# Three more seven-product quads in a hybrid attention and SSM block, and one set of operands fetched by another queue

## The chip, the cores and the metric

The kernel runs on one core of a Trainium2 chip. Its time is the device time of one execution in microseconds (us), the median of several runs. The core has a matrix engine (TensorE, PE in the profile; its weight loads are PEld), a vector engine (VectorE, DVE), a scalar engine (ScalarE, ACT), GpSimd (POOL) and SyncE (SP), which here only issues DMA transfers. Each engine works through its own list of instructions in order.

## What is computed

A block with two branches over 256 positions and a model width of 2048, in float32. Shortened from the reference:

```python
hn = rms_norm(x, norm_w)
q, k, v, z_a, z_s, xbc, dt_raw, g_a, g_s = split(hn @ w_in)
o_a = dilated_window_attention(q, k, v) * silu(z_a)      # 16 heads of 128
y   = rms_norm(ssd_scan(conv(xbc), dt_raw) * silu(z_s), ssm_norm_w)
merged = sigmoid(g_a) * (o_a @ w_attn_branch) + sigmoid(g_s) * (y @ w_ssm_branch)
out = rms_norm(x + merged @ w_out, final_norm_w)
```

Attention scores get a bias that grows with the distance between two positions, and the exponentials are weighted by how many of the three window patterns hold a pair: two constant tables, `dist` and `count`.

## The kernel before

Each large product is made of float32 operands that are split in two parts of lower precision, a high and a low one, and of three matmuls: high by high, high by low, low by high. Weights stream from HBM in units of 128x1024 numbers (512 KB) into a ring of five buffers. For a unit `w`, ACT writes the high part `h` (line 278) and DVE the low part `l = w - h` (line 279).

The work runs in stages: gate of the SSM branch, SSM heads and scan (`ps_xs`, `ps_zs`), the SSM branch product (`ps_ssm`), value projection (`ps_v`), 16 attention heads (`ps_q`, `ps_k`, `ps_za`), then the gate of the attention branch (`ps_ga`), the attention branch product (`ps_attn`) and the output product (`ps_out`). The products ssm, v, ga, attn and out are made by `gemm_pair` (line 463 on), in two passes each, named by the columns that they start with, 0 and 2. A pass for ga, attn or v has eight *quads* of two 128-row tiles each. A plain quad takes two units and 24 matmuls of 512 columns. A quad that is listed in `S_QUADS` is made by the seven-product scheme of Strassen and Winograd instead: seven block products of three matmuls, 21 in all. `G_ORDERS`, `V_ORDERS` and `A_ORDERS` give the order of the quads of a pass.

A seven-product quad needs other operands than a plain one:

- a whole unit `wa`, half a unit `wc`, and a table `wt` of block differences, which was made earlier and put into HBM. On ACT there are four high parts, `ha`, `hc`, `htt` and `htu` (line 551). On DVE there are their low parts `la`, `lc`, `ltt`, `ltu` (line 552) and one subtraction in place, `wa - wt` (line 565), which `htu` and `ltu` are made of.
- left factors: sums of blocks of the left operand, split in two. They are made once per quad (`keep_left`), stored in HBM (`spill`, line 242) and fetched back (`fetch_left`, line 441). `sx_x` are those of the input, used by v and ga; `sx_o` are those of the attention output, used by attn. The buffer in which a left factor of the attention output is made, `sxt_o`, has the tag "ht", as has the high part `htu`, and there are two buffers of that tag.

The tables `wt` for ga, attn and out are made during the attention heads by `sum_jobs` (line 244 on): each job loads 768 KB, makes two DVE subtractions of 128x512 (lines 254, 255) and stores 512 KB. Here there are 19 jobs, started at every fourth unit. A small copy by POOL (lines 249, 253, 440) makes a transfer wait for a chosen unit.

All transfers of weights, tables and left factors are issued on SP's queue, in its order. After the eight quads of a pass, `fold` (lines 589 to 594) combines four of the products; for ga, two tanh passes follow, and for attn, DVE adds and scales the results (lines 1155, 1144, 1145), before PE transposes them (`mtp`, line 1137). The order of the instructions on each engine is set by a scheduler, from priorities in the code.

Of the kernel before, what the change touches and what calls it, by code (L numbers as in the profile page):

```python
# [23 lines left out]
KT = D // P  # L24
# [12 lines left out]
DT_LAG, CB_LAG, TURN_LAG, GT_LAG, Y_LAG, S_LAG, M_LAG = 2, 8, 3, 2, 11, 2, 2  # L37
Y_AFTER = 0, 0
GS_BEFORE = {0: (0, 1), 4: (2,)}
A_ORDERS = {0: (0, 1, 2, 4, 3, 6, 5, 7), 2: (0, 2, 1, 4, 3, 5, 6, 7)}  # L40
V_ORDERS = {0: (0, 2, 4, 1, 3, 5, 6, 7), 2: (0, 2, 1, 4, 3, 5, 6, 7)}
G_ORDERS = {c: (0, 2, 1, 4, 3, 5, 6, 7) for c in (0, 2)}
O_LEFT = {0: {0: (0, 3), 4: (1, 5)}, 2: {}}
O_ORDERS = {0: (0, 1, 2, 4, 3, 6, 5, 7), 2: None}
RX_UNITS = {c: 16 + c for c in range(1, 8)}
# [2 lines left out]
NEG = -1.0e30  # L48
S_QUADS = {
    ("ssm", 0): (5, 7, 8, 10, 11, 12, 13), ("ssm", 2): (3, 5, 7, 8, 10, 11, 12, 13),  # L50
    ("v", 0): (2, 3, 4, 5, 6), ("v", 2): (2, 4, 5, 6), ("ga", 0): (2, 4, 5, 6), ("ga", 2): (2, 4, 5, 6),
    ("attn", 0): (2, 4, 6), ("attn", 2): (2, 4, 5, 6), ("out", 0): (3, 5), ("out", 2): (3, 5),
}
Y_ORDERS = {0: (0, 1, 2, 3, 5, 4, 7, 8, 6, 10, 11, 9, 12, 14, 13, 15), 2: (0, 3, 1, 5, 2, 7, 8, 4, 10, 11, 6, 12, 9, 13, 14, 15)}
Y_LATE = {12: 4, 13: 6}
SX_Y = sorted({*S_QUADS[("ssm", 0)], *S_QUADS[("ssm", 2)]}, key=Y_ORDERS[0].index)
Y_SPARE = {q: int(q in S_QUADS[("ssm", 0)] and q in S_QUADS[("ssm", 2)]) for q in SX_Y}
SX_X = (2, 4, 5, 6)
SX_V = (3,)
O_BEHIND = 7, 14, 15, 17  # L60
SUMS_ATT = [(t, q) for t in [(n, c) for n in ("ga", "attn", "out") for c in (0, 2)] for q in S_QUADS[t]]
ATT_QUADS = sorted({*S_QUADS[("attn", 0)], *S_QUADS[("attn", 2)]})
IN_PLACE = {"ssm": [(0, 12), (2, 12)]}
SUMS_SSM = [(t, q) for t in (("ssm", 0), ("ssm", 2), ("v", 0), ("v", 2)) for q in S_QUADS[t] if (t[1], q) not in IN_PLACE.get(t[0], ())]
SUM_UNITS = 2, 9, 16
LEFT_EVERY, ATT_EVERY = 11, 4
SUM_LAG = 3
ROOM_SSM = 2
WHOLE = slice(0, 512)
# [129 lines left out]
def hybrid_block(ctx: ExitStack, tc: tile.TileContext, wall, xt, x, pk_d, cst_d, fw_d, out):  # L199
# [34 lines left out]
    def behind_unit(n, f):  # L234
        on_unit.setdefault(n, []).append(f)
# [56 lines left out]
    def blocks(t, c):  # L292
        return [t[:, i, (c + j) * 512 : (c + j + 1) * 512] for i in range(2) for j in range(2)]
# [140 lines left out]
    def new_sx(pool, bufs, spare, name):  # L434
        return pool.tile([P, 2, 4 - spare, P], F32R, name=f"sx_{name}", tag=f"sx{spare}", bufs=bufs)

    def fetch_left(kept, pool, bufs, key, x, spare, u):
        def get(behind):
            sx = new_sx(pool, bufs, spare, f"{key[0]}{key[1]}")
            gp.tensor_copy(sx[:, 0, 0, 0:1], behind)  # L440
            nc.sync.dma_start(sx.bitcast(F32), lefts[key])
            kept[key[1]] = left_parts(sx, x, spare)

        behind_unit(u, get)
# [140 lines left out]
    def fold(prods, dst):  # L585

        d11, d12, d21, d22 = dst
        p1, p5, p6, p7 = prods
        ac.activation(d11, p1, AF.Copy)
        ac.activation(d22, p5, AF.Copy)  # L590
        ve.tensor_tensor(d12, p6, d11, ALU.add)
        ve.tensor_tensor(d21, p7, d12, ALU.add)
        ve.tensor_tensor(d12, d12, d22, ALU.add)
        ve.tensor_tensor(d22, d21, d22, ALU.add)
# [4 lines left out]
            ac.activation(th[:, i, tag[1] * 512 : tag[1] * 512 + 512], accs[i], AF.Tanh, scale=scales[i])  # L599

    def rsqrt_rows(sums, n, name):
        var = lead.tile([P, 2], F32, name=f"var_{name}", tag="var", bufs=1)
        ve.tensor_scalar(var, sums, 1.0 / n, EPS, ALU.mult, ALU.add)
        r = lead.tile([P, 2], F32, name=f"r_{name}", tag="rr", bufs=1)
        gp.tensor_tensor(r, var, half, ALU.pow)
        hr = lead.tile([P, 2], F32, name=f"hr_{name}", tag="hr", bufs=1)
        ve.tensor_scalar(hr, r, 0.5, None, ALU.mult)
        return r, hr

# [83 lines left out]
    with tc.tile_pool(name="ssm", bufs=2) as sp:  # L693
# [327 lines left out]
    vt = big.tile([P, 2, D], F32, name="vt", tag="yo1a")  # L1021
    th_a = big.tile([P, 2, D], F32, name="th_a", tag="yo1b")
    xl = ctx.enter_context(tc.tile_pool(name="xl", bufs=1))
    dc = xl.tile([P, 768], F32, name="dc", tag="dc")
    dist_c, count_c = dc[:, :384], dc[:, 384:]
    behind_unit(FIRST[("v", 2)] + 1, lambda behind: fetch(dc, cst_d[:, :768], behind))
    room = room_of(big.tile([P, 6 * 512], F32, name="room_v", tag="yo0a"), 2, 2)
    with tc.tile_pool(name="vx", bufs=1) as vx:
        tl = big.tile([P, 4, UNIT], F32R, name="tl_v", tag="yo0b")
        room["tl"] = [(tl[:, 2 * n], tl[:, 2 * n + 1]) for n in range(2)]  # L1030
        for n, q in enumerate(SX_V):
            fetch_left(sx_of_x, vx, len(SX_V), ("x", q), two_kts(XT, q), 0, FIRST[("v", 0)])
        for n, q in enumerate(SX_X[1:]):
            fetch_left(sx_of_x, xl, len(SX_X) - 1, ("x", q), two_kts(XT, q), 0, FIRST[("v", 0)] + 1 + n)
        for c in (0, 2):
            es, prods = gemm_pair(
                ("v", c), lambda kt: XT[:, kt, :], KT, sx_of_x, c == 2, order=V_ORDERS[c], room=room
            )
            dst = blocks(vt, c)
            fold(prods, dst)  # L1040
            for d, e in zip(dst, es):
                ve.tensor_tensor(d, e, d, ALU.add)
    sx_of_o = {}

    with tc.tile_pool(name="att", bufs=2) as ap:
# [4 lines left out]
        def scores(h, q, k, p):  # L1050
            sps = bank("m1", 2, f"sps{h}")
            pe.matmul(sps[:, :P], q[:, :P], k[:, :P], start=True, stop=True)
            pe.matmul(sps[:, P:384], q[:, P:], k, start=True, stop=True)
            t = cpool.tile([P, 384], F32, name=f"t{h}", tag="ssq")
            slope = 2.0 ** (-8.0 * (h + 1) / NH)
            ve.scalar_tensor_tensor(t, dist_c, slope / SCALE, sps[:, :384], ALU.mult, ALU.add)
            st = ap.tile([P, 8], F32, name=f"st{h}", tag="st", bufs=1)
            parts = ((0, P), (P, 384))
            for i, (a, b) in enumerate(parts):
                ve.tensor_reduce(st[:, i : i + 1], t[:, a:b], mybir.AxisListType.X, ALU.max)  # L1060
            ve.tensor_scalar(st[:, 2:4], st[:, 0:2], -SCALE, None, ALU.mult)
# [17 lines left out]
        def mix(h, pT, za):  # L1079
# [204 lines left out]
```

## Time and profile before

| | |
|---|---|
| time, median of 3 runs | 1381.65 us (1379.74 to 1382.66) |
| the profiled execution | 1381.59 us, its span 1379.8 us |
| PE busy | 1368.4 us, 99% of the span |
| DVE busy | 1168.4 us, 85% |
| ACT busy | 836.6 us, 61% |
| POOL busy | 142.5 us, 10% |
| granted TensorE clock | full in all 40 slices of the span |

The profile shows one execution. A busy time is the time in which an engine has an instruction in work. In timelines, an instruction's start and length are given, and in square brackets how long its engine had been idle before it and what ended the idle time. A matmul's length there is its whole latency; matmuls overlap, so their price is the distance between two starts.

### The profile page before, as it was taken

How to read it: one execution, taken by the hardware profiler on the slowest of the kernel's cores; microseconds unless marked ns; L12 is line 12 of the kernel's file. 1: busy time of each engine (PE TensorE's matmuls, PEld its weight loads, DVE VectorE, ACT ScalarE, POOL GpSimd, SP SyncE). 2: the span in 40 equal slices, each digit the busy share in tenths (PEclk: the TensorE clock that was granted, in tenths of full speed). 3: DMA queues.
4: the chain of work that ended last, by engine and by line, in shares of the span. 5: the costliest groups of instructions: out<-in, count | busy, mean ns of one | idle time of the engine just before them, and what ended most of it. 6: DMA issues, size and time to landing. Idle time of an engine off the chain costs nothing.

```text
span 1379.8 us, 20706 instructions
## 1 busy us (share of the span) xinstructions
PE 1368.4 (99%) x7266; PEld 1166.4 (85%) x7266; DVE 1168.4 (85%) x1753; ACT 836.6 (61%) x1306; POOL 142.5 (10%) x226
## 2 busy tenths in 40 slices
PE   9999999999999999999999999999999999999997
PEld 7888888888888888888888888888888888888886
DVE  6897999897899898788989887777877788888997
ACT  7655777675667676666565554454445556655554
POOL 2301111101010100010001001211111000000112
PEclk9999999999999999999999999999999999999999
DMA  9766978778787867578677668888888757875773
GB/s 348 232 193 198 334 261 284 263 245 283 249 278 236 302 200 223 175 240 277 228 259 273 209 218 282 280 275 276 289 288 300 241 163 268 290 224 177 247 271 122
DMA packets 105080, 345.00 MB, mean 250 GB/s; under 512 B 11728, under 2 KB 13712, under 8 KB 104976
## 3 DMA queue, kind: packets, MB, share of 16 engines
q1 hardware_dynamic: 103536, 339.62, 73.7%
q10 hardware_dynamic: 1440, 4.06, 0.8%
q8 instruction: 57, 0.93, 0.3%
q14 instruction: 47, 0.39, 0.1%
HBM read 314.87 MB, written 28.77 MB: 249 GB/s over the span
## 4 chain that ended last, share of the span: by engine, by line
PE 95%; DMA 2%; ACT 1%; issue 1%; DVE 1%; SPq 0%; POOL 0%; POOLq 0%; ACTq 0%; DVEq 0%
PE ps_xs L333 8%; PE ps_zs L333 8%; PE ps_za L333 4%; PE ps_k L333 4%; PE ps_q L333 4%; PE ps_xs L339 4%; PE ps_zs L339 4%; PE ps_ssm L485 3%; PE ps_ssm L486 3%; PE ps_ssm L484 3%; PE ps_q L339 2%; PE ps_k L339 2%; PE ps_za L339 2%; PE ps_gs L421 2%; PE ps_gs L422 2%; PE ps_gs L420 2%
## 5 line engine op out<-in xcount | busy, mean ns | idle before, releaser
L278 ACT ACTIVATE h<-w 128x1024 fp32r<-128x1024 f32 (+1 forms) x398 | 413.8, 1047 | 303.9 <-issue 80.9
L279 DVE TENSOR_TENSOR l<-w,h 128x1024 fp32r<-128x1024 f32 (+1 forms) x398 | 478.8, 1209 | 114.0 <-ACT h L278 110.4
L333 PE MATMUL ps_zs<-XT,h 128*128 128x512 f32 x496 | 172.1, 393 | 0.0
L333 PE MATMUL ps_xs<-XT,h 128*128 128x512 f32 x496 | 171.6, 393 | 0.0
L339 PE MATMUL ps_zs<-XT,l 128*128 128x256 f32 x496 | 134.8, 280 | 0.9 <-DVE l L279 0.9
L339 PE MATMUL ps_xs<-XT,l 128*128 128x256 f32 x496 | 133.7, 277 | 0.0
L333 PEld LDWEIGHTS ps_xs<-XT,h 128*128 128x128 f32 x496 | 91.3, 188 | 19.4
L333 PEld LDWEIGHTS ps_zs<-XT,h 128*128 128x128 f32 x496 | 91.3, 188 | 18.8
L339 PEld LDWEIGHTS ps_zs<-XT,l 128*128 128x128 f32 x496 | 93.3, 188 | 3.7 <-DVE l L279 1.6
L339 PEld LDWEIGHTS ps_xs<-XT,l 128*128 128x128 f32 x496 | 93.2, 188 | 2.1
L333 PE MATMUL ps_q<-XT,h 128*128 128x512 f32 x256 | 91.1, 404 | 0.0
L333 PE MATMUL ps_k<-XT,h 128*128 128x512 f32 x256 | 88.6, 395 | 0.0
L333 PE MATMUL ps_za<-XT,h 128*128 128x512 f32 x256 | 88.4, 394 | 0.0
L551 ACT ACTIVATE ha<-wa 128x1024 fp32r<-128x1024 f32 x43 | 45.4, 1055 | 43.6 <-PE ps_ssm L486 12.9
L339 PE MATMUL ps_q<-XT,l 128*128 128x256 f32 x256 | 68.4, 278 | 0.0
L339 PE MATMUL ps_k<-XT,l 128*128 128x256 f32 x256 | 68.4, 277 | 0.0
L339 PE MATMUL ps_za<-XT,l 128*128 128x256 f32 x256 | 68.4, 277 | 0.0
L792 ACT ACTIVATE gt<-acb,acT 128x128 f32<-128x128 f32 x128 | 44.0, 391 | 28.8 <-DMA acb<-acum_d 27.4
L552 DVE TENSOR_TENSOR la<-wa,ha 128x1024 fp32r<-128x1024 f32 x43 | 52.4, 1219 | 9.3 <-ACT ha L551 9.2
L552 DVE TENSOR_TENSOR ltu<-wa,htu 128x1024 fp32r<-128x1024 f32 x38 | 46.3, 1219 | 15.9 <-ACT htu L551 15.9
L333 PEld LDWEIGHTS ps_k<-XT,h 128*128 128x128 f32 x256 | 47.0, 188 | 9.9
L333 PEld LDWEIGHTS ps_q<-XT,h 128*128 128x128 f32 x256 | 47.1, 188 | 9.7
(688 smaller groups left out, 3315.1 us busy)
## 6 DMA issues: line engine op xcount, KB each, us to landing
w<-in_wall SPq DMA_DIRECT2D x394, 512.0 KB, 4.8
wa<-in_wall SPq DMA_DIRECT2D x43, 512.0 KB, 5.1
th_a<-in_wall SPq DMA_DIRECT2D x19, 512.0 KB, 5.6
sums_at<-in_wall SPq DMA_DIRECT2D x18, 512.0 KB, 4.7
acb<-acum_d SPq DMA_DIRECT2D x32, 256.0 KB, 3.8
t_ssm<-sums_at SPq DMA_DIRECT2D x13, 512.0 KB, 4.8
wt<-t_ssm SPq DMA_DIRECT2D x13, 512.0 KB, 4.7
th_a<-in_wall SPq DMA_DIRECT2D x19, 256.0 KB, 6.2
```

The lines of the kernel that those rows point to most:

```text
L278: ac.activation(h[:, a:b], w[:, a:b], AF.Copy)
L279: ve.tensor_tensor(l[:, a:b], w[:, a:b], h[:, a:b].bitcast(F32), ALU.subtract)
L333: high = pe.matmul(acc, h[:, kk, :], xs_of(kt), start=(kt == 0), stop=False)
L339: low = pe.matmul(acc[:, S:], l[:, kk, :], xs_of(kt)[:, :S], start=False, stop=(kt == KT - 1))
L420: pe.matmul(accs[i], xh, h[:, kk], start=(kt == 0), stop=False)
L421: pe.matmul(accs[i], xh, l[:, kk], start=False, stop=False)
L484: pe.matmul(acc, xh, h, start=start, stop=False)
L485: pe.matmul(acc, xh, l, start=False, stop=False)
L486: pe.matmul(acc, xl, h, start=False, stop=stop)
L551: ac.activation(h, src, AF.Copy)
L552: ve.tensor_tensor(l, src, h.bitcast(F32), ALU.subtract)
L792: ac.activation(g4[:, n, b], acb[:, j, b // 2 * P : b // 2 * P + P], AF.Relu, scale=-1.0, bias=sc[:, h : h + 1],)
```

## The change

- Three more quads go by the seven-product scheme: quad 3 in both passes of ga, and quad 5 in the first pass of attn. The order of the quads in ga becomes 0, 2, 4, 1, 3, 5, 6, 7 (it was 0, 2, 1, 4, 3, 5, 6, 7), which is the order of the first pass of v in both kernels. In the first pass of attn, quad 5 comes ahead of quad 6.
- The left factor of input quad 3 was used by v alone and had a buffer of its own; now it is kept with the others until the end of ga.
- There are 22 `sum_jobs` in place of 19, started at every 3.75 units from unit 3 on (every 4 from unit 7 on before).
- The four fetches of `sx_o` are issued on GpSimd's queue, and the first of them behind an earlier unit of ga's second pass.
- The constant tables of the attention scores lie in places of constants that are no longer needed, in three transfers, in place of one buffer of 768 columns.

```diff
-A_ORDERS = {0: (0, 1, 2, 4, 3, 6, 5, 7), 2: (0, 2, 1, 4, 3, 5, 6, 7)}
+A_ORDERS = {0: (0, 1, 2, 4, 3, 5, 6, 7), 2: (0, 2, 1, 4, 3, 5, 6, 7)}
-G_ORDERS = {c: (0, 2, 1, 4, 3, 5, 6, 7) for c in (0, 2)}
+G_ORDERS = {c: (0, 2, 4, 1, 3, 5, 6, 7) for c in (0, 2)}
...
-    ("v", 0): (2, 3, 4, 5, 6), ("v", 2): (2, 4, 5, 6), ("ga", 0): (2, 4, 5, 6), ("ga", 2): (2, 4, 5, 6),
-    ("attn", 0): (2, 4, 6), ("attn", 2): (2, 4, 5, 6), ("out", 0): (3, 5), ("out", 2): (3, 5),
+    ("v", 0): (2, 3, 4, 5, 6), ("v", 2): (2, 4, 5, 6), ("ga", 0): (2, 3, 4, 5, 6), ("ga", 2): (2, 3, 4, 5, 6),
+    ("attn", 0): (2, 4, 5, 6), ("attn", 2): (2, 4, 5, 6), ("out", 0): (3, 5), ("out", 2): (3, 5),
...
-SX_X = (2, 4, 5, 6)
-SX_V = (3,)
-O_BEHIND = 7, 14, 15, 17
+SX_X = (2, 4, 3, 5, 6)
+O_BEHIND = 3, 14, 15, 17
...
-    def fetch_left(kept, pool, bufs, key, x, spare, u):
+    def fetch_left(kept, pool, bufs, key, x, spare, u, queue=nc.sync):
         def get(behind):
             sx = new_sx(pool, bufs, spare, f"{key[0]}{key[1]}")
             gp.tensor_copy(sx[:, 0, 0, 0:1], behind)
-            nc.sync.dma_start(sx.bitcast(F32), lefts[key])
+            queue.dma_start(sx.bitcast(F32), lefts[key])
...
-    dc = xl.tile([P, 768], F32, name="dc", tag="dc")
-    dist_c, count_c = dc[:, :384], dc[:, 384:]
-    behind_unit(FIRST[("v", 2)] + 1, lambda behind: fetch(dc, cst_d[:, :768], behind))
+    count = lead.tile([P, P], F32, name="count", tag="cw"), cst[:, 512:768]
+    for n, (dst, a) in enumerate(((mask3, 0), (count[0], 384), (count[1], 512))):
+        behind_unit(FIRST[("v", 2)] + n, lambda behind, dst=dst, a=a: fetch(dst, cst_d[:, a : a + dst.shape[-1]], behind))
...
-            SUMS_ATT, range(FIRST[("q", 0)] + 7, N_UNITS, ATT_EVERY),
+            SUMS_ATT, [FIRST[("q", 0)] + 3 + n * 15 // 4 for n in range(len(SUMS_ATT))],
...
-                sx_of_o, xl if n else xk, max(1, n and len(SX_X) - 1), ("o", q), two_kts(oaT, q), 0, FIRST[("ga", 2)] + O_BEHIND[n]
+                sx_of_o, xl if n else xk, max(1, n and len(SX_X) - 1), ("o", q), two_kts(oaT, q), 0, FIRST[("ga", 2)] + O_BEHIND[n], nc.gpsimd
```

PE's list is the same up to quad 2 of ga's first pass, and 9 rows shorter in all. The first place is there: PE at the end of quad 2, whose last two operands are `htu_11637` before and `htu_11660` after (`ha`, `la`, `hc`, `lc` belong to quad 4; `h`, `l` to quad 1; line numbers are one less after the change). Before:

```order
L485 MATMUL pp_ga_0_11615<-la_11710,XT 128x512
L486 MATMUL pp_ga_0_11615<-ha_11709,XT 128x512
L485 MATMUL ps_ga_0_11527<-la_11710,XT 128x512
L486 MATMUL ps_ga_0_11527<-ha_11709,XT 128x512
L485 MATMUL ps_ga_1_11528<-lc_11714,sx_x_7835 128x512
L486 MATMUL ps_ga_1_11528<-hc_11713,sx_x_7835 128x512
L484 MATMUL pp_ga_3_11618<-htu_11637,sx_x_7640 128x512
L484 MATMUL ps_ga_2_11529<-htu_11637,XT 128x512
L485 MATMUL pp_ga_3_11618<-ltu_11638,sx_x_7640 128x512
```

And after:

```order
L484 MATMUL ps_ga_3_11553<-l_11737,XT 128x512
L485 MATMUL ps_ga_3_11553<-h_11736,XT 128x512
L483 MATMUL ps_ga_0_11550<-h_11742,XT 128x512
L483 MATMUL ps_ga_1_11551<-h_11742,XT 128x512
L483 MATMUL ps_ga_3_11553<-h_11742,XT 128x512
L483 MATMUL pp_ga_3_11641<-htu_11660,sx_x_7636 128x512
L483 MATMUL ps_ga_2_11552<-htu_11660,XT 128x512
L484 MATMUL ps_ga_0_11550<-l_11743,XT 128x512
```

From the first matmul behind the last transpose (`ptp`) of the heads, `htu` of quad 2 comes in the 31st place before and in the 25th after.

The second place is DVE at the end of attn's first pass, where the folded products (`fin`) and the operands of the second pass meet. Before, the list reads (`ltt_12693` and all below it that is named `la` or `ltu` belongs to the second pass):

```order
L552 TENSOR_TENSOR ltu_12492<-wa_12474,htu_12491 128x1024
L279 TENSOR_TENSOR l_12519<-w_12516,h_12518 128x1024
L279 TENSOR_TENSOR l_12525<-w_12522,h_12524 128x1024
L591 TENSOR_TENSOR fin<-pp_attn_2_12352,fin 128x512
L279 TENSOR_TENSOR l_12555<-w_12552,h_12554 128x1024
L279 TENSOR_TENSOR l_12561<-w_12558,h_12560 128x1024
L592 TENSOR_TENSOR fin<-pp_attn_3_12353,fin 128x512
L552 TENSOR_TENSOR ltt_12693<-fin,htt_12692 128x1024
```

And after (`ltt_12736` and `la_12727` belong to the second pass):

```order
L278 TENSOR_TENSOR l_12604<-w_12601,h_12603 128x1024
L551 TENSOR_TENSOR ltt_12567<-fin,htt_12566 128x1024
L278 TENSOR_TENSOR l_12685<-w_12682,h_12684 128x1024
L551 TENSOR_TENSOR ltu_12571<-wa_12553,htu_12570 128x1024
L278 TENSOR_TENSOR l_12691<-w_12688,h_12690 128x1024
L590 TENSOR_TENSOR fin<-pp_attn_2_12389,fin 128x512
L1150 TENSOR_TENSOR fin<-ps_attn_0_12308,fin 128x512
L591 TENSOR_TENSOR fin<-pp_attn_3_12390,fin 128x512
L551 TENSOR_TENSOR ltt_12736<-fin,htt_12735 128x1024
L1139 SCALAR_TENSOR_TENSOR th_a<-th_a,fin 128x512
L592 TENSOR_TENSOR fin<-fin 128x512
L551 TENSOR_TENSOR la_12727<-wa_12722,ha_12726 128x1024
```

Before, the low parts of two plain quads stand ahead of the fold; after, the last parts of a seven-product quad do, and the fold and the sums of the pass are woven between the operands of the next one.

The third place is the fetch of the left factors `sx_o`. Before, SP's list has them between weights:

```order
L530 DMA wa_12167<-in_wall 128x1024
L441 DMA sx_o_12097<-sxd_o_9995 128x1024
L534 DMA wc_12169<-in_wall 128x512
L267 DMA w_12210<-in_wall 128x1024
L267 DMA w_12219<-in_wall 128x1024
L267 DMA w_12275<-in_wall 128x1024
L267 DMA w_12281<-in_wall 128x1024
L441 DMA sx_o_12216<-sxd_o_10780 128x1024
L267 DMA w_12314<-in_wall 128x1024
```

After, they stand in POOL's list, each behind its small copy:

```order
L439 CAST sx_o_12091<-h_12087 128x1
L440 DMA sx_o_12091<-sxd_o_10005 128x1024
L439 CAST sx_o_12253<-h_12249 128x1
L440 DMA sx_o_12253<-sxd_o_10794 128x1024
L439 CAST sx_o_12262<-h_12258 128x1
L440 DMA sx_o_12262<-sxd_o_11191 128x1024
```

Four transfers have left SP's list, and what stands behind them there no longer comes after the copies by POOL.

## Rows read from the trace of the kernel before

**Rows 1.** The page: busy time, share of the span and instructions of each engine.

```profile
PE 1368.4 (99%) x7266; PEld 1166.4 (85%) x7266; DVE 1168.4 (85%) x1753; ACT 836.6 (61%) x1306; POOL 142.5 (10%) x226
```

**Rows 2.** Waits of PE over the whole span: us in total, times, longest.

```profile
PE warm L631 <- DVE ssq L628: 1.4, 1, 1.4
PE ps_zs L339 <- DVE l L279: 0.9, 2, 0.8
PE ps_first L385 <- ACT h L278: 0.7, 2, 0.4
```

**Rows 3.** Chain that ended last, gate's second pass: start, us, what.

```profile
1169.55 0.68 PE ps_ga L484 x3
```

**Rows 4.** Windows: stretch, then us, PE, PEld, DVE, ACT, POOL busy, PEclk, DMA share, GB/s.

```profile
745.10:786.10 41.00, 41.00 (x183) 33.95 (x182) 36.98 (x40) 23.59 (x28) 3.29 (x3) 1.00 0.71 247
...
800.00:1126.80 326.80, 326.80 (x1862) 285.40 (x1861) 250.69 (x465) 165.64 (x250) 43.83 (x57) 1.00 0.78 261
1126.80:1165.00 38.20, 38.20 (x172) 31.68 (x171) 32.23 (x33) 22.03 (x27) 0.00 (x0) 1.00 0.76 248
1165.00:1206.20 41.20, 41.20 (x184) 34.12 (x183) 36.81 (x40) 27.77 (x33) 2.12 (x4) 1.00 0.87 306
1206.20:1247.00 40.80, 40.80 (x182) 33.80 (x181) 35.14 (x40) 20.84 (x24) 0.00 (x0) 1.00 0.68 213
```

**Rows 5.** DVE's timeline, gate's first pass: start, us, line, operation, idle before.

```profile
1134.65 2.35 DVE L279 TENSOR_TENSOR l<-w,h 128x1024 fp32r<-128x1024 f32 x2
1136.92 1.22 DVE L552 TENSOR_TENSOR ltu<-wa,htu 128x1024 fp32r<-128x1024 f32 x1
1138.06 1.22 DVE L552 TENSOR_TENSOR la<-wa,ha 128x1024 fp32r<-128x1024 f32 x1
1139.20 0.68 DVE L552 TENSOR_TENSOR lc<-wc,hc 128x512 fp32r<-128x512 f32 x1
1139.80 1.22 DVE L552 TENSOR_TENSOR ltt<-th_a,htt 128x1024 fp32r<-128x1024 f32 x1
1140.93 1.22 DVE L565 TENSOR_TENSOR wa<-wa,th_a 128x1024 f32<-128x1024 f32 x1
```

**Rows 6.** ACT's timeline there: `htu` of quad 2.

```profile
1131.16 1.06 ACT L551 ACTIVATE htu<-wa 128x1024 fp32r<-128x1024 f32 x1 [3.04 <-DMA sxd_o<-sxt_o]
```

**Rows 7.** PE's timeline there: the first matmul that reads `htu` of quad 2.

```profile
1133.58 0.39 PE L484 MATMUL pp_ga<-htu,sx_x 128*128 128x512 f32 x1
```

**Rows 8.** SP's timeline there: the store of the last left factor of o.

```profile
1126.73 0.33 SPq L242 DMA_DIRECT2D sxd_o<-sxt_o  x1
```

**Rows 9.** ACT's timeline at the start of attn's second pass.

```profile
1249.80 1.04 ACT L551 ACTIVATE htu<-wa 128x1024 fp32r<-128x1024 f32 x1
```

**Rows 10.** PE's timeline there: the first matmul that reads this `htu`.

```profile
1251.67 0.40 PE L484 MATMUL ps_attn<-htu,oaTa 128*128 128x512 f32 x1
```

**Rows 11.** The page: DVE groups of the sum jobs, busy us, mean ns, idle before.

```profile
L254 DVE TENSOR_TENSOR th_a<-th_a 128x512 f32<-128x512 f32 x19 | 13.2, 693 | 1.5
L255 DVE TENSOR_TENSOR th_a<-th_a 128x512 f32<-128x512 f32 x19 | 13.1, 690 | 0.4
```

**Rows 12.** DMA issues in 1165 to 1206.2: count, KB each, median us to landing.

```profile
w<-in_wall SPq DMA_DIRECT2D x10, 512.0 KB, 5.8
...
sx_o<-sxd_o SPq DMA_DIRECT2D x4, 512.0 KB, 6.0
```

**Rows 13.** Waits of SP's queue, 1120 to 1210: us in total, times, longest.

```profile
SPq L441 <- POOL sx_o L440: 5.0, 3, 2.3
```

**Rows 14.** POOL's timeline from gate's second pass on: start, us, operation, idle before.

```profile
1188.67 1.24 POOL L440 CAST sx_o<-h 128x1 fp32r<-128x1 f32 x1 [11.37 <-ACT h L278]
...
1198.48 0.18 POOL L440 CAST sx_o<-h 128x1 fp32r<-128x1 f32 x1 [7.43 <-PE pp_ga L486]
1279.90 3.16 POOL L646 COPY fin<-h 128x1 f32<-128x1 f32 x1 [81.25 <-ACT h L278]
```

**Rows 15.** SP's timeline: the first fetch of a left factor of o.

```profile
1177.33 0.33 SPq L441 DMA_DIRECT2D sx_o<-sxd_o  x1
```

**Rows 16.** PE's timeline: the first matmul that reads one.

```profile
1213.14 0.39 PE L484 MATMUL ps_attn<-hc,sx_o 128*128 128x512 f32 x1
```

More of the change, by code (lines that the diff above doesn't have):

```diff
@@ L65 @@
 SUM_UNITS = 2, 9, 16
-LEFT_EVERY, ATT_EVERY = 11, 4
+LEFT_EVERY = 11
 SUM_LAG = 3
@@ L601, in rsqrt_rows @@
     def rsqrt_rows(sums, n, name):
-        var = lead.tile([P, 2], F32, name=f"var_{name}", tag="var", bufs=1)
+        rows = lead.tile([P, 3, 2], F32, name=f"rows_{name}", tag="rows", bufs=1)
+        var, r, hr = rows[:, 0], rows[:, 1], rows[:, 2]
         ve.tensor_scalar(var, sums, 1.0 / n, EPS, ALU.mult, ALU.add)
-        r = lead.tile([P, 2], F32, name=f"r_{name}", tag="rr", bufs=1)
         gp.tensor_tensor(r, var, half, ALU.pow)
-        hr = lead.tile([P, 2], F32, name=f"hr_{name}", tag="hr", bufs=1)
         ve.tensor_scalar(hr, r, 0.5, None, ALU.mult)
@@ L916, in left_x @@
             keep_left(("x", q), two_kts(XT, q), 0, at)
-        for n, q in enumerate(SX_X + SX_V):
+        for n, q in enumerate(SX_X):
             behind_unit(begin + 3 + n * LEFT_EVERY, lambda behind, q=q: left_x(q, behind))
@@ L1023, in hybrid_block @@
     xl = ctx.enter_context(tc.tile_pool(name="xl", bufs=1))
-    dc = xl.tile([P, 768], F32, name="dc", tag="dc")
-    dist_c, count_c = dc[:, :384], dc[:, 384:]
-    behind_unit(FIRST[("v", 2)] + 1, lambda behind: fetch(dc, cst_d[:, :768], behind))
+    count = lead.tile([P, P], F32, name="count", tag="cw"), cst[:, 512:768]
+    for n, (dst, a) in enumerate(((mask3, 0), (count[0], 384), (count[1], 512))):
+        behind_unit(FIRST[("v", 2)] + n, lambda behind, dst=dst, a=a: fetch(dst, cst_d[:, a : a + dst.shape[-1]], behind))
     room = room_of(big.tile([P, 6 * 512], F32, name="room_v", tag="yo0a"), 2, 2)
[L1028 to L1042, printed above, removed]
+    tl = big.tile([P, 4, UNIT], F32R, name="tl_v", tag="yo0b")
+    room["tl"] = [(tl[:, 2 * n], tl[:, 2 * n + 1]) for n in range(2)]
+    for n, q in enumerate(SX_X[1:]):
+        fetch_left(sx_of_x, xl, len(SX_X) - 1, ("x", q), two_kts(XT, q), 0, FIRST[("v", 0)] + n)
+    for c in (0, 2):
+        es, prods = gemm_pair(
+            ("v", c), lambda kt: XT[:, kt, :], KT, sx_of_x, c == 2, order=V_ORDERS[c], room=room
+        )
+        dst = blocks(vt, c)
+        fold(prods, dst)
+        for d, e in zip(dst, es):
+            ve.tensor_tensor(d, e, d, ALU.add)
     sx_of_o = {}
@@ L1055, in scores @@
             slope = 2.0 ** (-8.0 * (h + 1) / NH)
-            ve.scalar_tensor_tensor(t, dist_c, slope / SCALE, sps[:, :384], ALU.mult, ALU.add)
+            ve.scalar_tensor_tensor(t, mask3, slope / SCALE, sps[:, :384], ALU.mult, ALU.add)
             st = ap.tile([P, 8], F32, name=f"st{h}", tag="st", bufs=1)
@@ L1065, in scores @@
                 ve.scalar_tensor_tensor(
-                    p[:, a:b], p[:, a:b], 1.0, count_c[:, a:b], ALU.mult, ALU.mult,
+                    p[:, a:b], p[:, a:b], 1.0, count[i], ALU.mult, ALU.mult,
                     accum_out=st[:, 4 + i : 5 + i],
```

## The prediction

> **What bounds the kernel now.** I began with the busy times of the page: PE is busy for 1368.4 us, 99% of the span, DVE for 85% [rows 1]. The question is then whether PE's work has gaps. The list of PE's waits has 3.0 us in the whole span, 1.4 us on the sum of squares and 1.6 us on split weights, none of it in value, gate, attention or output products [rows 2]. The windows say the same of the three passes that the change touches: in 1126.8 to 1247 PE is busy for all of each window, at full clock [rows 4]. So here the time of a stage is its number of matmuls times their distance. The chain of work that ended last gives that distance: three matmuls of 512 columns in 0.68 us, 0.2267 us each [rows 3].
>
> DVE is the engine behind it. In the three windows it is busy for 32.23 of 38.20, 36.81 of 41.20 and 35.14 of 40.80 us [rows 4], so it stands idle for 5.97, 4.39 and 5.66 us. A matmul removed is worth its 0.2267 us only as long as the operands of the next still come in time. That is what has to be costed.
>
> **The change part by part.** The profiled execution took 1381.59 us, 1.8 us more than its span and 0.06 under the median, so the sum made against it stands for the median too.
>
> *Matmuls.* A plain quad has 24 and a seven-product quad 21. Three quads change: 9 matmuls less, 9 x 0.2267 = 2.04 us. PE's list is shorter by exactly these 9 rows. If no operand comes late, this is the whole gain.
>
> *DVE.* Two low parts of a plain quad take from 1134.65 to 1136.92, 2.27 us. In a seven-product quad, `la`, `lc` and `ltt` take from 1138.06 to 1140.93, 2.87 us, and `wa - wt` and `ltu` 1.14 us each (the distance from `ltu` at 1136.92 to the next start): 5.15 us [rows 5]. Each of the three quads thus adds 2.88 us to DVE and takes 0.68 us from PE. In the windows that leaves DVE idle for 5.97 - 2.88 - 0.68 = 2.41 us in gate's first pass, 0.83 in its second and 2.10 in attention's first. It still fits, barely in gate's second pass. In gate's new order three seven-product quads follow each other (3, 5, 6): DVE 3 x 5.15 = 15.45, PE 3 x 4.76 = 14.28 us, so DVE falls back by 1.17 us in them. The nearest row is the first pass of v, which has the same five quads in the same order: DVE 36.98 of 41.00 us, PE busy throughout [rows 4]. It kept 4.02 us of idle time, more than any of the three will have, so it speaks for the change without settling it.
>
> *Quad 2 of gate's first pass.* This is the tightest place that I found. `htu` runs from 1131.16 to 1132.22 on ACT, and ACT had stood 3.04 us before it until the store of the last left factor of o had landed, since both use a buffer of tag "ht" [rows 6]. PE reads it at 1133.58 [rows 7], a lead of 1.36 us. After the change its place is the 25th and not the 31st, six matmuls or 1.36 us earlier: PE comes at 1132.22, and the lead is nought. The store is issued at 1126.73 [rows 8] behind a split that stands behind the same DVE work after the change, so it has no reason to move. It took some 4.4 us; were it to take the 5.8 us that a weight takes in a crowded window [rows 12], PE would stand for 1.4 us. Bounds 0 to 1.4, and I take 0.2, since the store's own row is the nearest.
>
> *Gate's second pass.* In its crowded window weights take 5.8 us to land [rows 12], and only 0.83 us of DVE's idle time remain. If none of DVE's idle time there can be used, because each piece of it stands before something that was late, the pass loses 2.88 + 0.68 = 3.56 us less a lead such as the 1.36 us above: bounds 0 to 2.2. I take 0.4, nearer to v's pass, which lost nothing.
>
> *End of attention's first pass.* Quad 5 now is a seven-product quad next to the end, and the fold is woven between the second pass's operands. Before, `htu` of the second pass is done at 1250.84 [rows 9] and read at 1251.67 [rows 10], a lead of 0.83 us. By the same reckoning the bounds are 0 to 3.56 - 0.83 = 2.73; I take 0.4, since 2.10 us of idle time remain.
>
> *Sum jobs.* Three more of them are 3 x (0.693 + 0.690) = 4.1 us on DVE [rows 11] over a stretch where it is idle for 76 of 326.8 us [rows 4], with three stores and six loads. Nothing on PE's path; if that cover were gone, 4.1 us. The three added tables must be read back as well: that is in the load of the windows, 0.25 MB a quad.
>
> *Left factors by GpSimd.* SP's queue stood 5.0 us at three of these fetches, with weights queued behind [rows 13]; PE had no wait there, so freeing it gives back nothing by itself, only slack in the gate's second pass. What a fetch issued by GpSimd costs no row shows. POOL's last copy for them is at 1198.48, and its next work at 1279.90 [rows 14], so what the queue takes itself is hidden; fetches took 6.0 us [rows 12], and the first of these factors, asked for at 1177.33 [rows 15], is first read at 1213.14 [rows 16], 36 us later, so several us more are hidden. Bounds: nothing, or DVE held back as long as the longest of these small POOL instructions, 1.24 us [rows 14], four times, 5.0 us. I take nothing.
>
> By the Trainium skill, DMA: Bandwidth & Descriptors, Issuing engine by pattern, fetches by Sync are "generally faster" than by GpSimd, with a first byte some 0.4 us earlier by its specifications; the sum would be the same by it, since 36 us lie between. No run here shows it yet.
>
> *Tables and constants* move three small transfers and no arithmetic: nothing, with cover of the whole v pass.
>
> Sum: 1381.59 - 2.04 + 0.2 + 0.4 + 0.4 = 1380.55, as a number 1380.5 us; with no stall at all 1379.55.
>
> **The rivals.**
>
> *DVE's idle time cannot be used (slower).* Place: the three passes. In each, DVE's chain grows by 2.88 us and PE's shrinks by 0.68; if the idle time stays where it is, each pass loses 3.56 us less the lead that it had: 10.68 - 1.36 - 1.36 - 0.83 = 7.1 us. Time: 1381.59 - 2.04 + 7.1 = 1386.7. It decides against the change from 2.04 us of stalls on, and measurably from 4.8 us. For it: idle of only 0.83 us in the second gate window, and waits there on DMA and buffers, as before `htu`. Against it: v's first pass with the same quads, without a wait.
>
> *GpSimd's fetches hold DVE (slower).* 5.0 us as above less the 0.83 us left idle: 1380.55 + 4.2 = 1384.7. For it, that nothing in this trace has been issued so; against it, that POOL's small copies lie beside running DVE work without a mark on it.
>
> The Trainium skill, GPSIMD Engine Reference, SBUF interfaces, speaks against the change here: GpSimd shares them with VectorE, which suffers when it reads two SBUF inputs, as every low part does. How long descriptor work would hold it, no run shows.
>
> *More than the matmuls (faster).* The two waits of `ps_zs`, 0.9 us [rows 2], lie in the heads where left factors and their store move. If they vanish and nothing stalls: 1381.59 - 2.04 - 0.9 = 1378.65, over 0.2%. Against it: nothing in the change aims at them.
>
> That the change doesn't do what it says is left out: PE's list is 9 rows shorter.
>
> **How the numbers follow.** Less than 0.2% (2.76 us) can't be told from no change here. Forecast, stalls of 0 to 2.7 us, 1379.5 to 1382.3: 0.67, within 0.2%. Idle time that cannot be used, in whole or from 4.8 us on: 0.15, and GpSimd's fetches: 0.05; both slower. More than the matmuls, or a median of three that falls low (the runs before spread over 2.9 us): 0.13, faster. So faster 0.13, same 0.67, slower 0.20. The range goes from 1378.6, the faster rival, to 1385.5, which takes in the second rival and the lower half of the first.
>
> **What would show it.** Right: PE's waits in the new trace stay near 3.0 us plus 1.0, all three windows have PE busy throughout, shorter by 0.68 us each, DVE's idle time in them falls to some 2.4, 0.8 and 2.1 us, and `htu` of quad 2 is read as soon as it is done. Wrong: waits of PE on `ltu`, `la` or `l` of over 2 us in a pass (the first rival); low parts longer than 1.23 us around 1172 to 1200 (the second); a wait on `sx_o`; or waits in the attention heads, where the sum jobs lie.

## The result, and the profile after

The changed kernel takes 1386.74 us, the median of 6 runs (1384.70 to 1388.11), against 1381.72 us (1379.74 to 1382.66) for the kernel before. The ratio is 1.0037, with a 95% interval of 1.0026 to 1.0047: slower by 5.0 us, where 1.2 us less was forecast. The time lies outside the range that was given (1378.6 to 1385.5), and next to the first rival's 1386.7.

The page of the profiled execution (1386.18 us, span 1384.2) begins with the engines' busy times, as [rows 1]; the second line is the new DMA queue in its part 3 (packets, MB, share).

```profile
PE 1368.9 (99%) x7257; PEld 1164.5 (84%) x7257; DVE 1181.0 (85%) x1768; ACT 841.6 (61%) x1312; POOL 155.4 (11%) x241
...
q0 software_dynamic: 576, 2.10, 0.4%
```

PE has its 9 instructions less (7257 for 7266), and four fetches, 2.10 MB, now go by another kind of queue. The list of PE's waits, as [rows 2], tells where the loss is:

```profile
PE ps_attn L484 <- DVE l L278: 1.7, 1, 1.7
PE warm L629 <- DVE ssq L626: 1.4, 1, 1.4
PE ps_first L384 <- ACT h L277: 1.2, 2, 0.8
PE ps_attn L483 <- ACT hc L550: 1.2, 1, 1.2
PE ps_out L483 <- ACT fin L588: 0.7, 1, 0.7
PE ps_zs L338 <- DVE l L278: 0.7, 1, 0.7
PE ps_attn L483 <- ACT h L277: 0.4, 1, 0.4
```

Four of these are new: three on operands of the attention product, one at the start of the output product. Next come the windows, as [rows 4], with one more for the start of attn's second pass:

```profile
1126.80:1165.00 38.20, 38.13 (x171) 31.25 (x170) 34.63 (x36) 24.75 (x29) 0.00 (x0) 1.00 0.76 245
1165.00:1206.00 41.00, 40.98 (x181) 33.62 (x180) 38.85 (x42) 28.40 (x34) 13.60 (x8) 1.00 0.90 311
1206.00:1247.00 41.00, 41.00 (x182) 33.95 (x182) 35.86 (x38) 24.38 (x29) 0.00 (x0) 1.00 0.70 224
1247.00:1262.00 15.00, 11.67 (x56) 8.62 (x55) 13.30 (x18) 5.56 (x7) 0.00 (x0) 1.00 0.49 176
```

In the gate's passes and in attention's first pass PE is busy throughout, as before. Then, in 15 us around the start of attention's second pass, it is idle for 3.3 us. DVE's idle time in the three passes is 3.57, 2.15 and 5.14 us, where 2.4, 0.8 and 2.1 were forecast: in attention's first pass DVE has hardly more to do than before, and in the 15 us behind it, it is busy for 13.30.

Why the operands are late there is told by DVE's timeline. Where does the first of the folds begin (line 591 before, 590 after)? Before:

```profile
1230.76 0.68 DVE L591 TENSOR_TENSOR fin<-pp_attn,fin 128x512 f32<-128x512 f32 x1
```

After, with the instruction ahead of it, and the two low parts for which PE waits:

```profile
1236.81 1.22 DVE L278 TENSOR_TENSOR l<-w,h 128x1024 fp32r<-128x1024 f32 x1
1239.80 0.69 DVE L590 TENSOR_TENSOR fin<-pp_attn,fin 128x512 f32<-128x512 f32 x1 [1.77 <-PE pp_attn L485]
...
1250.55 2.35 DVE L278 TENSOR_TENSOR l<-w,h 128x1024 fp32r<-128x1024 f32 x2
```

A fold needs the last product of the last seven-product quad. Before, that quad was the third from the end, so most of fold and merge found room while PE worked on two plain quads. Now it is the second from the end: the fold begins 9.0 us later, after DVE has stood for 1.77 us, and then DVE is busy without a gap up to the late `l`, with the 4 folds, 4 sums, 3 of the 8 merges (lines 1139 and 1140 after the change) and the next pass's operands. PE reads the first `l` at 1251.81, when it is just done.

The second wait comes about in another way, which the chain that ended last shows (start, us, what):

```profile
1254.03 1.04 DVE th_a L1139 x2
1255.08 4.92 DMA fin<-in_wall
...
1260.10 0.64 ACT hc L550
```

The half unit `wc` of the second pass is loaded into 512 columns of `fin`, where a result of the first pass lies until it is merged (line 1139). The late merge makes a late transfer, and PE waits for `hc`.

The third place is ACT's timeline at the end of attention:

```profile
1283.33 1.05 ACT L550 ACTIVATE htu<-wa 128x1024 fp32r<-128x1024 f32 x1
1286.52 0.35 ACTq L645 DMA_DIRECT2D fin<-in_x  x1
1286.91 0.60 ACT L588 ACTIVATE fin<-pp_attn 128x512 f32<-128x512 f32 x1 [2.54 <-POOL fin L644]
```

ACT's copy in the fold of the second pass now stands behind a transfer of `x` that ACT issues itself, and that one waits for a small copy by POOL. Before, the copy stood ahead of it. The output product needs the bank that the copy empties.

The distances between PE's starts, less the usual one of the instruction, give the sum: 2.04 us less for nine matmuls; 4.2 us more at the boundary between attention's passes (1.90, 1.40 and 0.72 on the three waits above, 0.20 on a `lc`); 0.9 at the start of the output product; 0.4 in two waits in the gate; 0.6 at the very start, where the first weights came later; 0.8 in small pieces; 0.5 less at the end. Together 4.4 us, the difference of the two spans.

### The profile page after: what moved, and what is told of

It reads as the page before. It is cut to its first block, busy times and chain, and to the rows that moved or that the text cites. A ratio compares the mean times of both kernels' runs of the same rounds, so it can differ in the third digit from the quotient of the medians.

```text
span 1384.2 us, 20755 instructions
## 1 busy us (share of the span) xinstructions
PE 1368.9 (99%) x7257; PEld 1164.5 (84%) x7257; DVE 1181.0 (85%) x1768; ACT 841.6 (61%) x1312; POOL 155.4 (11%) x241
## 4 chain that ended last, share of the span: by engine, by line
PE 93%; DMA 2%; issue 2%; DVE 1%; ACT 1%; POOL 0%; SPq 0%; POOLq 0%; ACTq 0%; DVEq 0%
PE ps_xs L332 8%; PE ps_zs L332 8%; PE ps_za L332 4%; PE ps_k L332 4%; PE ps_q L332 4%; PE ps_xs L338 4%; PE ps_zs L338 4%; PE ps_ssm L484 3%; PE ps_ssm L485 3%; PE ps_ssm L483 3%; PE ps_q L338 2%; PE ps_k L338 2%; PE ps_za L338 2%; PE ps_gs L420 2%; PE ps_gs L421 2%; PE ps_gs L419 2%
## 5 line engine op out<-in xcount | busy, mean ns | idle before, releaser
L277 ACT ACTIVATE h<-w 128x1024 fp32r<-128x1024 f32 (+1 forms) x392 | 407.9, 1047 | 302.8 <-issue 67.2
L278 DVE TENSOR_TENSOR l<-w,h 128x1024 fp32r<-128x1024 f32 (+1 forms) x392 | 471.8, 1209 | 105.7 <-ACT h L277 102.7
L550 ACT ACTIVATE ha<-wa 128x1024 fp32r<-128x1024 f32 x46 | 48.6, 1057 | 51.4 <-DMA wa<-in_wall 10.2
L551 DVE TENSOR_TENSOR la<-wa,ha 128x1024 fp32r<-128x1024 f32 x46 | 56.1, 1219 | 13.4 <-ACT ha L550 13.2
L551 DVE TENSOR_TENSOR ltu<-wa,htu 128x1024 fp32r<-128x1024 f32 x41 | 50.0, 1219 | 11.3 <-ACT htu L550 11.3
```

The lines of the kernel that those rows point to most:

```text
L277: ac.activation(h[:, a:b], w[:, a:b], AF.Copy)
L278: ve.tensor_tensor(l[:, a:b], w[:, a:b], h[:, a:b].bitcast(F32), ALU.subtract)
L550: ac.activation(h, src, AF.Copy)
L551: ve.tensor_tensor(l, src, h.bitcast(F32), ALU.subtract)
```

## The experiments

Each was timed beside the kernel before on the same chip; ratios are against it, with 95% intervals. Waits that are given *by PE's starts* are such distances. Theory A says that the loss is at the end of attention's first pass, by the place of its last seven-product quad. The letters of the rivals are in the expectations, and "..." in an edit stands for the part of a line that stays.

### The attention quad taken back (two samples)

```diff
-A_ORDERS = {0: (0, 1, 2, 4, 3, 5, 6, 7), ...
+A_ORDERS = {0: (0, 1, 2, 4, 3, 6, 5, 7), ...
...
-    ("attn", 0): (2, 4, 5, 6), ...
+    ("attn", 0): (2, 4, 6), ...
```

> The changed kernel with the first pass of attn as it was before the change (quads 2, 4, 6 by seven products, 5 plain, order 6, 5, 7 at its end); the rest of the change stays, so 6 matmuls less than before, 1.36 us. Theory A (all that matters is at the end of attn's first pass): the waits of PE of 4.2 us at 1248 to 1262 and the one of 0.9 us at the start of out vanish, and the time is 1381.7 - 1.4 + 0.4 (the two small waits in gate) = 1380.7. Theory B (what costs is in gate or the GpSimd fetches or the sum jobs, and the wait in attn is only where it shows): the waits move but stay, 1384 to 1387.

> The same kernel as in the first experiment (gate's quads and GpSimd's fetches, attn's first pass as before), once more beside the kernel before, for a narrower interval: six matmuls less, 1.36 us, and one wait of 0.2 us in gate; ratio 0.9992 if nothing else is lost.

1381.06 us, ratio 0.9995 (0.9987 to 1.0004), and the second time 1381.73 us, 0.9996 (0.9987 to 1.0005). PE's waits in the second sample are all:

```profile
PE warm L629 <- DVE ssq L626: 1.4, 1, 1.4
PE ps_first L384 <- ACT h L277: 0.9, 2, 0.7
```

No wait in attention is left, nor the one at the output product, in either sample. The loss of 5 us hangs on this one quad. Six matmuls less should give 1.36 us; by their ratios both samples lie on that side, by 0.5 to 0.7 us, and neither is clear of no change. That this kernel beats the one before isn't shown.

### The attention quad alone

```diff
-A_ORDERS = {0: (0, 1, 2, 4, 3, 6, 5, 7), ...
+A_ORDERS = {0: (0, 1, 2, 4, 3, 5, 6, 7), ...
...
-    ("attn", 0): (2, 4, 6), ...
+    ("attn", 0): (2, 4, 5, 6), ...
```

> The kernel before with one edit: quad 5 of attn's first pass by seven products, ahead of quad 6, with its one sum job; 3 matmuls less than before, 0.68 us. Theory A: this edit alone makes the loss, PE waits of 4 to 5 us on l and hc at the start of attn's second pass, 1385 to 1386. Theory B: no more than 1382.

1384.38 us, ratio 1.0021 (1.0012 to 1.0030). Its waits in attention:

```profile
PE ps_attn L484 <- ACT htu L551: 1.2, 1, 1.2
PE ps_attn L484 <- ACT hc L551: 1.0, 1, 1.0
...
PE ps_attn L485 <- DVE l L279: 0.2, 1, 0.2
```

The same place, and the same two ways, at a smaller size than expected: 1.0021 is 2.9 us, and the time lies below Theory A's 1385 to 1386. The edit is slower by itself, without gate, left factors or queue. The rest of the loss comes only in the company of the other parts: by PE's starts the boundary costs 3.0 us here and 4.2 in the changed kernel, and the wait at the output product isn't here.

### Two plain quads last

```diff
-A_ORDERS = {0: (0, 1, 2, 4, 3, 5, 6, 7), ...
+A_ORDERS = {0: (0, 1, 2, 4, 5, 6, 3, 7), ...
```

> The changed kernel with the same four seven-product quads in attn's first pass, but in the order 0, 1, 2, 4, 5, 6, 3, 7: two plain quads behind the last seven-product one and not one. Theory A1 (the place of the last seven-product quad matters, since the fold can't start before it and its results must be merged before the second pass gets its buffers for wc): the fold starts some 5.4 us earlier against the end of the pass, the waits of 4.2 us fall below 1 us, 1381 to 1383. Theory A2 (five more DVE operations in the pass, wherever they stand): the waits stay, within 1 us of the changed kernel, 1386 to 1387.5.

1384.38 us, ratio 1.0019 (1.0010 to 1.0029): between the two expectations, some 2.4 us better than the changed kernel and 2.6 worse than the one before. By PE's starts the waits at the boundary are 2.1 us in place of 4.2. The fold begins at 1237.82 and not at 1239.80, 2 us earlier and not 5.4. These are DVE's timeline at it, and ACT's for the instruction that DVE waits for:

```profile
1236.67 1.23 DVE L551 TENSOR_TENSOR ltu<-wa,htu 128x1024 fp32r<-128x1024 f32 x1 [2.51 <-ACT htu L550]
1237.82 0.68 DVE L590 TENSOR_TENSOR fin<-pp_attn,fin 128x512 f32<-128x512 f32 x1
```

```profile
1235.58 1.06 ACT L550 ACTIVATE htu<-wa 128x1024 fp32r<-128x1024 f32 x1 [2.67 <-PE ps_attn L485]
```

DVE waits for ACT, and ACT for PE, which has to read an older part before its buffer can be written. So these 2.51 us of DVE's idle time can't be spent on the operands ahead, and the fold stands behind them in DVE's list. Both answers hold a part: the place of the last quad, and work that can't be done ahead.

### The seven-product quads earlier

```diff
-A_ORDERS = {0: (0, 1, 2, 4, 5, 6, 3, 7), ...
+A_ORDERS = {0: (0, 2, 1, 4, 5, 6, 3, 7), ...
```

> The kernel with the three mends, but with attn's first pass in the order 0, 2, 1, 4, 5, 6, 3, 7. If an earlier start of the seven-product quads lets DVE come ahead, the waits at the boundary (2.1 us) fall to 1 us, 1382.5 to 1383. If DVE can't come ahead because high and low parts wait for buffers that PE has to read first, they stay, 1383.5 to 1384.5.

1383.95 us, ratio 1.0019 (1.0010 to 1.0028), against 1.0017 (1.0008 to 1.0025) for the order that it was taken from (three mends, below). An earlier start of the quads gives nothing that the time shows, as it must if DVE can't come ahead; by PE's starts the waits at the boundary are 1.6 us, where the three mends have 2.1, and not the 1 us of the other answer. Whether more buffers would let DVE come ahead was not run.

### A place of its own for `wc`

```diff
-        room = {... "wc": [fin[:, i, :512] for i in range(2)]}
+        room = {... "wc": [t[:, i] for t in [fp.tile([P, 2, 512], F32, name="wcs", tag="wcs", bufs=1)] for i in range(2)]}
```

> The changed kernel with one edit: the half units wc of both attn passes get two buffers of their own in place of quarters of fin, which the first pass's results use until they are merged. Theory A (two waits: the low part l that stands in DVE's list behind fold and merges, and wc, which could be fetched only behind the merge): the waits on hc and h at 1260 to 1262 (2.1 us) vanish, the one on l (1.9 us) shrinks to 1.0 to 1.5, since the list is woven anew; 1383.5 to 1384.7. Rival (the DVE list is the only limit): the wait moves to the next operand, 1386 to 1387.

1385.43 us, ratio 1.0027 (1.0016 to 1.0037); by the medians 1.3 us better than the changed kernel, where 2.0 to 3.2 were expected, and the two intervals overlap. The trace tells more: by PE's starts the boundary costs 2.9 us in place of 4.2. The wait on `hc` is gone, but those on DVE's list remain or moved to the next operands, and one turned up in the gate that no theory had:

```profile
PE ps_attn L483 <- ACT htu L550: 1.2, 1, 1.2
PE pp_ga L483 <- ACT ha L550: 1.0, 1, 1.0
PE ps_attn L484 <- DVE ltu L551: 0.8, 1, 0.8
```

So the transfer was one of two limits, and the list of DVE the other. The wait in the gate comes with this edit: the three kernels that have it wait 1.0 to 1.1 us there, the others 0.2 us or less. In this kernel's chain the unit `wa` that `ha` is made of takes long:

```profile
1170.83 5.73 DMA wa<-in_wall
```

SP issues it right behind the two fetches of `wc`, which now come at 1169.17, and it takes 5.7 us to land; weights in the same stretch of the changed kernel took 4.3. That the two fetches slow it is likely, but was not shown.

### The merges left out

```diff
-                    merge(c + n % 2, n // 2, dst[n])
+                    if c:
+                        merge(c + n % 2, n // 2, dst[n])
```

> The changed kernel with the eight merge operations of attn's first pass left out (lines 1139 and 1140: gate times product, and sum with the SSM branch, for the first half of the columns), so half of the merged columns lack the attention branch. It takes 4.8 us of DVE work from the boundary, 1.2 us of it ahead of the first late low part l, and lets wc be fetched before any merge. Theory A (DVE's list of fold, sums and merges is what makes l late, and the merge is what makes wc late): waits of 4.2 us at the boundary fall to 1 us or less, 1383.0 to 1383.9 with the 0.9 us at out's start. Rival (the quad's own work or the buffers of the high and low parts set the wait, whatever stands in the list): 1385.5 and over.

1383.50 us, ratio 1.0009 (1.0000 to 1.0018). Not one wait in attention is left; what remains beside the start is at the output product:

```profile
PE ps_out L483 <- ACT fin L588: 1.4, 1, 1.4
PE ps_out L483 <- ACT h L277: 0.2, 1, 0.2
```

With eight DVE operations fewer at the boundary, and `wc` no longer behind a merge, the same four seven-product quads in the same order cost no wait there. The price is the DVE work between the fold's start and the next pass's operands, and what hangs on it. The edit takes both ways away at once; how much is the transfer's, the place of its own for `wc` tells better.

### The first fetch of x later

```diff
-X_BEHIND = (("out", 0), 1), ...
+X_BEHIND = (("out", 0), 2), ...
```

> The changed kernel with one edit: the first fetch of x for out behind the next unit, so that ACT's copy in the fold of attn's second pass stands ahead of it. If the wait of 0.9 us at out's start is this place in ACT's list, it vanishes and nothing else moves: 1385.8. If it only shows how late the second pass is, it stays: 1386.7.

1385.65 us, ratio 1.0028 (1.0017 to 1.0038), and no wait of the output product in the trace. That wait was the place of one copy in ACT's list, worth 0.9 us by the trace; the times agree, but the two intervals overlap.

### Three mends together

> The changed kernel with three edits: own buffers for wc, attn's first pass in the order 0, 1, 2, 4, 5, 6, 3, 7, and the first fetch of x for out behind the next unit, so that ACT's copy in the fold of attn's second pass no longer stands behind a transfer that waits for a copy by POOL. Theory A: the wait of 0.9 us at out's start vanishes, those at the boundary fall to 1.0 or less: 1386.7 - 0.9 - 3.2 = 1382.6, and 1381 if the boundary is free. Rival (DVE's work in the pass is too much in any order): 1384 and over.

The edits are three of those shown above: an own place for `wc`, the order 0, 1, 2, 4, 5, 6, 3, 7, and the first fetch of x later. 1383.76 us, ratio 1.0017 (1.0008 to 1.0025). The waits at the boundary remain with 0.6, 1.0 and 0.5 us between PE's starts, on `l` and `ltu`, and the one in the gate is there too. The time lies between the two expectations, and it is still slower than the kernel before: with this quad, mending the places doesn't pay for the DVE work.

### The fetch of the left factors: SP or GpSimd

Three kernels: the changed one with SP's queue, the kernel before with GpSimd's, and the one with the gate's quads alone with SP's.

```diff
-                sx_of_o, ... FIRST[("ga", 2)] + O_BEHIND[n], nc.gpsimd
+                sx_of_o, ... FIRST[("ga", 2)] + O_BEHIND[n]
```

> The changed kernel with the four fetches of o's left factors issued by SP again, behind the same units. If the fetch by GpSimd costs something (slower DVE, or the time that POOL needs), the time falls by 0.5 to 4 us; if it helps by keeping SP's queue free, it rises by 0.5 to 2 us; if it is hidden either way, as predicted, it stays within 0.5 us of the changed kernel, 1386.2 to 1387.2.

> The kernel before, with only the four fetches of o's left factors issued by GpSimd (behind the same units as before). Theory A3 (the queue is worth something only where the passes have no slack left): no wait of PE in the passes before, none now, 1381.5 within 0.6 us. Theory B3 (a fetch on SP's queue costs the kernel by itself, and GpSimd's queue is a gain of its own): 1378 to 1380.5.

> The changed kernel without attn's quad and with the four fetches on SP's queue: the gate's two quads and SP fetches. Theory A3: the gate's quads have used up the slack, so SP's stand behind POOL's copies (11.2 us in the run with both) again brings weights late at the end of gate's second pass: PE waits of 2 to 4 us around 1199 to 1203 and 1 to 2 us of matmuls at half clock, 1383.5 to 1386. Rival: the loss of 4.4 us in that run came from having all three quads; then it stays at 1380.5 to 1382.

The changed kernel with SP's queue: 1391.16 us, ratio 1.0074 (1.0061 to 1.0086), 4.4 us slower than with GpSimd's, against every expectation but the second, and above its bound. The kernel before with GpSimd's queue: 1381.24 us, 0.9997 (0.9989 to 1.0006), no change. Gate's quads with SP's queue: 1384.68 us (1381.45 to 1390.30 in 12 runs), 1.0030 (1.0016 to 1.0043), against 0.9995 with GpSimd's. So the queue is worth nothing by itself, and by the medians 3.6 to 4.4 us (by the ratios 4.7 to 5.1) as soon as the gate has its two quads. The same wait of SP's queue stands in the traces of the first and the third, against the 5.0 us of [rows 13]; behind it is what PE waits for in the first:

```profile
SPq L440 <- POOL sx_o L439: 11.2, 3, 7.2
```

```profile
PE ps_attn L484 <- DVE l L278: 1.9, 2, 1.6
...
PE ps_attn L483 <- ACT h L277: 1.2, 2, 1.0
PE ps_attn L483 <- ACT th_a L588: 1.2, 1, 1.2
```

SP stands for 7.2 us in one piece behind a small copy of POOL, and the weights for attention's first pass come late by that: at the end of the gate PE stands for 3.0 us by its starts, in the first and in the third kernel alike. Of the 7.2 us, 4.0 are the copy itself, from 1189.24 on (it stands together with the next one below); in the kernel before it took 1.24 us [rows 14]. The last section shows what such a copy waits for. POOL's timeline, and the fetch in SP's:

```profile
1189.24 4.08 POOL L439 CAST sx_o<-h 128x1 fp32r<-128x1 f32 x2 [13.42 <-ACT h L277]
1193.22 0.33 SPq L440 DMA_DIRECT2D sx_o<-sxd_o  x1
```

The windows of the first kernel, at the end of the gate and at the boundary in attention, show one more thing:

```profile
1197.00:1202.50 5.50, 3.06 (x12) 1.69 (x11) 2.66 (x3) 3.79 (x5) 0.18 (x1) 1.00 0.99 384
1202.50:1206.00 3.50, 3.50 (x9) 2.75 (x9) 3.50 (x5) 1.21 (x3) 1.06 (x1) 0.51 0.80 287
...
1254.50:1257.20 2.70, 1.11 (x5) 0.69 (x5) 2.70 (x4) 1.01 (x1) 0.00 (x0) 1.00 0.71 258
1257.20:1260.60 3.40, 3.40 (x10) 2.66 (x9) 3.40 (x6) 0.00 (x0) 0.00 (x0) 0.50 0.84 217
```

Behind the first wait, in which PE was busy for 3.06 of 5.50 us, the granted clock is 0.51, the lower level of 1.2 GHz, and matmuls start 0.43 us apart for 3.5 us: some 1.6 us more. Behind the second, in which PE was busy for 1.11 of 2.70 us, the same comes again. So of what this kernel loses against the changed one, 3.3 us go with the clock and 3.0 with the waits at the end of the gate, while the boundary in attention costs 1.7 us less. The waits alone don't settle the clock: behind the same wait at the boundary of the changed kernel, and behind the same 3.0 us in the profiled execution of the third kernel, it stayed at 1.00.

The times of the third kernel divide by the granted clock over the span: the six executions with 0.998 or 0.999 took 1381.45 to 1384.00 us, the six with 0.996 or 0.997 took 1385.36 to 1390.30. So a good part of its 3.6 us goes with the clock too; why one execution loses clock and another doesn't is open.

## Why the prediction was wrong

**The matmuls** were right: PE's list is nine shorter. In the two samples without the attention quad the ratios have the right sign and some half of the size, without being clear of no change.

**The gate** was right. I took 0.2 and 0.4 us of waits for its two passes and found 0.2 and 0.2. The first pass of v was the proper row to lean on. In detail quad 2 came out better than reckoned: `htu` is done at 1131.10 and read at 1132.84, a lead of 1.74 us and not of nought, since the store before it took 2.6 us, not the 4.4 us that I kept.

**The end of attention's first pass** is the step that failed. I took 0.4 us and a bound of 2.73, and it costs 4.2 us, beyond the bound. The bound came from the DVE work of the pass against PE's time in it, less a lead. That left out two things that stand in the code and in the order that I had shown. A fold can't begin before the last seven-product quad is through, and by the change that quad came next to the end, so 16 operations of fold, sum and merge were put on the boundary: the first of them 9.0 us later, as DVE's timeline shows, and without the eight merges no wait at all. And `wc` is loaded into a place that only the merges make free, which is a second wait with a transfer's 4.9 us in it. I also took DVE's 2.10 us of idle time as a reserve. The run with two plain quads last shows 2.51 us of such time to be idle because ACT waits for PE's reading, so it can't be spent ahead; and in the changed kernel the pass has not 2.10 but 5.14 us of it, while PE waits behind the pass.

**The rival** of idle time that can't be used gave 1386.7 us, which meets the measured time by luck: it spread 7.1 us over three passes, and two of them lost almost nothing. Its mechanism holds in attention's pass alone, where the fold meets it. The sign that I named for it, over 2 us on `ltu`, `la` or `l` in a pass, didn't come (1.90 us on `l`); the waits on `hc` and `h` were not in my list.

**The left factors by GpSimd** were put at nothing, with the cover named (PE had no wait there). Alone that is right, 0.9997. Together with the gate's quads the same queue is worth 3.6 to 4.4 us: I had named the slack that it gives the gate's second pass, but costed the part against the trace of before, and not against the slack that the other parts of the change leave. That DVE would be held back by it (the second rival) isn't so: the low parts `l` in 1165 to 1206 take 1218 ns on average, with all four fetches in that stretch, and 1221 ns before. It is the small copies that are held, as the last section shows; I had seen no mark on them.

**The start of the output product**, 0.9 us, had no term at all. It comes from two instructions that changed places in ACT's list, far behind the edits.

## What to carry to other kernels

When work is added to a pass, look at the last thing that the next pass's buffers and operands wait for, and at where in the pass the closing work can begin; the mean load of an engine says little there. Idle time of a feeding engine is a reserve only where it isn't waiting for buffers that the fed engine has to empty. And cost each part of a change in the company of the others: a queue that was harmless with slack held the weights up as soon as the slack had been spent. A small copy that only orders a transfer isn't free either: in the changed kernel DVE's work held one for 5.2 us, and on SP's queue what stood behind such a transfer waited too.

## What the runs showed of the hardware

The DMA issues of the changed kernel in 1165 to 1206 (count, KB each, median us to landing):

```profile
w<-in_wall SPq DMA_DIRECT2D x9, 512.0 KB, 4.5
wa<-in_wall SPq DMA_DIRECT2D x5, 512.0 KB, 4.3
sx_o<-sxd_o POOLq DMA_DIRECT2D x4, 512.0 KB, 7.3
```

A fetch issued by GpSimd took 7.3 us where SP's of the same size took 4.3 to 4.5; issued by SP, in the kernel before, the same fetches took 6.0 us beside weights with 5.8 [rows 12]. That agrees with the Trainium skill, DMA: Bandwidth & Descriptors, Issuing engine by pattern, by which Sync's transfers are generally faster. It cost nothing here: PE has no wait on `sx_o`.

The Trainium skill, GPSIMD Engine Reference, SBUF interfaces, names contention between GpSimd and DVE's instructions with two SBUF inputs. Of DVE held by GpSimd the 1218 ns above show nothing for these four fetches; the small copies of the next rows agree with it the other way round, held by DVE.

POOL's copies of one column, which only order transfers, vary widely. POOL's timeline in the changed kernel, and DVE's where the first of these copies ends:

```profile
1175.98 5.17 POOL L439 CAST sx_o<-h 128x1 fp32r<-128x1 f32 x1 [101.87 <-PE pp_ga L485]
...
1194.15 0.47 POOL L439 CAST sx_o<-h 128x1 fp32r<-128x1 f32 x1
```

```profile
1181.73 1.23 DVE L551 TENSOR_TENSOR la<-wa,ha 128x1024 fp32r<-128x1024 f32 x1 [0.62 <-ACT ha L550]
```

The same work takes 5.17 us and 0.47 us, and what differs is DVE. The long copy ends at 1181.15, and DVE, which had been busy without a gap, has fallen idle at 1181.11. Behind the first 100 us the 14 traces have 2047 of these copies from `h`. Each of the 1461 that took over 0.2 us ends 0.04 to 0.05 us after the end of a DVE instruction; those that begin while DVE is idle take under 0.2 us. In the changed kernel all 106 such ends are of instructions that read two operands in SBUF, and the 15 copies that lie wholly inside one DVE instruction lie in ones that read an operand in PSUM, the matmuls' result memory. The profile's spans on POOL are rough, but the fetch that SP issues at 1193.22, in the kernel with SP's queue above, stands at such an end too: DVE's instruction ends at 1193.15. So the copies are held by DVE's instructions with two operands in SBUF, sometimes by several in a row. Why one copy comes in at the end of the running instruction and another only when DVE falls idle is open.

On SP's queue such a copy holds up the weights behind it. The third kernel of that experiment also had the widest spread of all, 8.9 us over 12 runs, where the others had 1.5 to 4.9. Its spread goes with the granted clock, as shown there; that the copies play a part in it was not shown.
